# Masks, first products and running sums written into PSUM by ScalarE, products added onto them by TensorE, and a new order of the work

## Chip, cores, metric

One core of one Trainium2 chip. The metric is the device time of one execution in microseconds (us): 423.28 before the change, the median of three runs (422.78 to 424.47).

## What is computed

A layer of an encoder, for 512 tokens of width 1024. Both branches and all gates start from the same normalised input; branch A is latent attention, branch B keeps the best 128 keys of each query by an indexer's scores.

```
h = rmsnorm(x, norm_g)
(q_lat, c_kv, k_rope, z_a, q_b, k_b, v_b, z_b, q_idx, k_idx, w_idx, gate_a, gate_b) = split(h @ w_in)
y_a = mla_attention(q_nope, q_pe, k_nope, k_pe, v_a, pos) * silu(z_a)          # 8 heads, chunk-causal
# branch B: score = sum_h relu(q_idx . k_idx) * w_idx; keys outside the top 128 or the later chunks drop out
logits = q_b . k_sel * scale + rel_bias[t5_bucket(key - query)]                # -inf where not valid
y_b = (softmax(logits) @ v_sel) * silu(z_b)                                    # 8 heads
merged = sigmoid(gate_a) * (y_a @ w_o_a) + sigmoid(gate_b) * (y_b @ w_o_b)
out = rmsnorm(x + merged @ w_out, final_g)
```

## The kernel before, in words

**Arithmetic.** Each fp32 operand is split into a high part, rounded by ScalarE (ACT, line 320 or 329), and a low part, the rest, made by VectorE (DVE, line 346) or GpSimd (POOL, line 348). A product of two operands is three matmuls onto one PSUM bank (`mm3`, line 422; all matmuls at line 418): high by high, low by high, high by low. There are 8 PSUM banks `ps`, each 128x512 fp32. Transposes are at line 435, branch A's logits at lines 1582 to 1584, the indexer's scores at line 883.

**Products in sevens.** Some 2x2 block products are made with seven half-size products in place of eight (`seven`, line 1105): two 512-wide projections as one pair (`proj2`, 84 matmuls of 256 columns in place of 48 of 512), branch B's values (`values2`, the tile `vv`) and the output product (`output`, line 1990, its right operands `s_wo` made by `out_job`). A plain 512-wide projection (`proj`) is 24 matmuls of 512 columns. Before, product 1 goes to SBUF and DVE makes the running sums: u2 is product 6 + product 1, u3 is product 7 added in the bank, then again + product 1; products 5 and 4 go to banks of their own and DVE adds them (`add`).

**Branch B's heads.** `dsa_base` loads a head's bias table and DVE (5 times POOL) adds each tile of `mask` to it, into the tile `s_p`. `mask` holds 0 or -1e30, is made from the top-128 search on DVE (lines 905, 906), and has widths 128 to 512 for the four query tiles. `dsa_head` makes the logits on TensorE into a fresh bank (`qhi` by `s_op`); one DVE instruction at line 1662 adds bank and `s_p` and takes the minimum of the negative; ACT takes the exponent; the rows are normalised, transposed (`s_ph`) and multiplied by `vv`.

**The order.** All engines run lists written at build time. `Flow` (line 140) is a planner: threads ask for steps, banks and slots; at each turn it issues the step that can start first by its own table of costs, with a preference for steps whose operands have been ready for some time (`SETTLE`, line 266), ties broken by a seeded draw (`DRAW`, line 264). `QUEUE` (line 2104) is the list of projection jobs: `ga`, `gb` gates, `za`, `zb`, `ma`, `pe`, `va`, `VB` values of branch B, `sb` its keys and queries, `ou` preparation of output operands; capital letters mean a product in sevens. `fetcher` loads their weights on SP's queue (SyncE) in this order, with four loads held back by `PASSED`; `splitter` splits them; `multiplier` issues the products. Two `lane` threads run the heads of each branch, two at a time. `branch_out` makes the sixteen outer projections (operands `s_ys`), `merged` the left operands `s_mg` of `output`; `finish`, `finish_twice` and `scale_out` do the last norm.

Of the kernel before, what the change touches and what calls it, by code (L numbers as in the profile page):

```python
# [43 lines left out]
class Buf:  # L44


    def __init__(self, tile, name):
        self.tile, self.name, self.w, self.r, self.written = tile, name, 0.0, 0.0, False
        self.by, self.reads = None, {}

    def __getitem__(self, idx):
        return View(self, self.tile[idx])
# [5 lines left out]

class View:
    def __init__(self, buf, ap):  # L60
        self.buf, self.ap = buf, ap

    def __getitem__(self, idx):
        return View(self.buf, self.ap[idx])
# [16 lines left out]
class Step:  # L81
# [4 lines left out]
    moves = 0.0  # L86
    pair = False
# [12 lines left out]
class Get:  # L100
    def __init__(self, pool, cls=None, cap=None):
        self.pool, self.cls, self.cap = pool, cls, cap
# [7 lines left out]
class Pool_:  # L110
# [5 lines left out]
    def give(self, req):  # L116
        if not self.free or (req.cap is not None and self.used.get(req.cls, 0) >= req.cap):
            return None
        self.free.sort(key=lambda b: max(b.w, b.r))
        self.used[req.cls] = self.used.get(req.cls, 0) + 1  # L120
        b = self.free.pop(0)
# [18 lines left out]
class Flow:  # L140
# [40 lines left out]
    def start(self, step, eng):  # L181
        s = self.free[eng]
        for b in step.ins:
            if not b.written and b not in step.outs:
                return math.inf
            s = max(s, b.w + (RAW_LAG.get(eng, 0.0) if b.by == eng else self.lat(b.by, eng)))
        for b in step.outs:
# [10 lines left out]
    def run(self, stop=None):  # L198
        while self.threads:
# [34 lines left out]
            if eng == "SP":  # L234

                self.free["SP"] = s + 0.05
                self.hw = max(self.hw, s) + (0.65 if step.ins and step.outs else 0.475)
                self.dma = max(self.dma, self.hw + 0.65)

                self.dma += dur * (SLOW if self.dma < 7.3 else 1.0)  # L240
                end = self.dma + (2.2 if step.ins and step.outs else 1.0) + step.late
            else:
# [7 lines left out]
                elif step.moves:  # L250
                    self.dma = max(self.dma, end + 1.0) + step.moves
                    end = self.dma + 1.0
            for b in step.ins:
                b.r = b.reads[eng] = max(b.r, end)
            for b in step.outs:
                b.w = max(b.w, end)
                b.written, b.by = True, eng
            self.advance(t, None)
# [5 lines left out]
DRAW = 53  # L264
# [6 lines left out]
def tile_block(ctx: ExitStack, tc: tile.TileContext, a: dict, out: bass.AP, bias_dram: bass.AP):  # L271
# [25 lines left out]
    ps_bufs = set(id(b) for b in PS.free)  # L297

# [6 lines left out]
    def bank(cls):  # L305
        return Get(PS, cls, {"mm": 3, "lg": 2, "pt": 2, "pv": 1, "e": 6}.get(cls))
# [105 lines left out]

    def mm(ps, pairs, start, stop, more=False):
# [6 lines left out]
        t = len(pairs) * (0.0133 + pairs[0][1].n / 2400)  # L420
        return pe(t, [ps], [v for p in pairs for v in p], emit, len(pairs))
# [8 lines left out]
    def turn(parts):  # L430
# [6 lines left out]
        return pe(0.107 * len(parts), [d for d, _ in parts], [s for _, s in parts] + [ident.all], emit, len(parts))  # L437

    held = []

    def hold(n, emit):

        return lambda: held.append([n, emit])

    def passed():
        for x in list(held):
            x[0] -= 1
            if not x[0]:
                held.remove(x)
                x[1]()  # L450

    def dma(dst, src):
# [5 lines left out]
        return Step([("SP", n / 360000.0, lambda: (nc.sync.dma_start(d, s), passed()))], bufs(dst), bufs(src))  # L458

    def pool_dma(dst, src):  # L460
        s = src.ap if isinstance(src, View) else src
        step = Step([("POOL", 1.03, lambda: nc.gpsimd.dma_start(dst.ap, s))], bufs(dst), bufs(src))
# [21 lines left out]
    def pool_dma_out(dst, src):  # L484
        step = Step([("POOL", 1.03, lambda: nc.gpsimd.dma_start(dst, src.ap))], [], bufs(src))
# [50 lines left out]
    def warm_up():  # L536
# [6 lines left out]
        for i in range(NWARM):  # L543
            step = pe(WARM, [ps.all], [zeros.all], fill(256))
            if i == NWARM - 1:
# [331 lines left out]
    def scores(i):  # L877
        n = P * (i + 1)
        work = mask[i]
        for h in range(NH):  # L880
            yield Until(lambda: h in qs and ks)
            ps = yield bank("lg")
            yield pe(0.005 + n / 2400, [ps.all], [qs[h].all, ks[0].all], lambda: nc.tensor.matmul(  # L883
                ps.tile[:, :n], qs[h].tile[:96, TOK[i]], ks[0].tile[:96, :n], start=True, stop=True))
            yield act(ps[:, :n], ps[:, :n], AF.Relu, scale=RD ** -0.5)
# [1308 lines left out]
```

## Time and profile before

| | |
|---|---|
| median of 3 runs | 423.28 us |
| the profiled execution, its time / its span | 422.78 us / 421.0 us |
| granted TensorE clock, mean | 0.996 |
| busy: PE (matmul) / DVE / ACT / POOL | 414.0 / 373.0 / 267.0 / 122.5 us |
| HBM traffic | 130 GB/s over the span |

PE is TensorE's matmuls, PEld its weight loads, SP the engine that issues most DMAs. A busy PE in the profile is a PE with matmuls in flight: their ends are modelled, so the pace of matmuls is better read from starts of long equal rows than from the busy share. In the rows of the timeline stand start, time, engine, line, operation, tiles and how many instructions were merged, and in square brackets the idle time of the engine before the first and who ended it. A tile's first letters name its use: `s_w` weights, `s_h` normalised input, `s_hs` its block sums, `s_pair` outputs of a pair, `s_xr` the residual.

### The profile page before, as it was taken

The numbers are of one execution on the slowest core, as the hardware profiler recorded it, in microseconds if no ns is written. First come the engines' busy times: TensorE is split into PE (matmuls) and PEld (weight loads), VectorE is DVE, ScalarE is ACT, GpSimd is POOL, SyncE is SP. The second block draws the span as 40 slices with busy tenths as digits, with TensorE's granted clock in tenths as the row PEclk, the third lists the DMA queues.
The fourth block names the chain that finished last, engine by engine and source line by source line (L and its number), as shares of the span: only waits on it lengthen the run. The fifth ranks groups of instructions, "written<-read, shape, count | busy, mean of one in ns | idle before, by whom it ended". The sixth has DMA issues, their size and how long they took to land.

```text
span 421.0 us, 7086 instructions
## 1 busy us (share of the span) xinstructions
PE 414.0 (98%) x2314; PEld 364.2 (87%) x2314; DVE 373.0 (89%) x801; ACT 267.0 (63%) x602; POOL 122.5 (29%) x135
## 2 busy tenths in 40 slices
PE   8999999999999999999999999999999999999994
PEld 7999888888888888888999988998998888888883
DVE  4789889569999999999999999979799758999995
ACT  5787778576764748625568677694598434436724
POOL 0037769543464659400013000200100000120650
PEclk9999999999999999999999999999999999999998
DMA  8983135665266341444652347245541888248305
GB/s 247 387 310 110 48 90 190 180 195 135 75 153 186 88 153 51 114 151 149 148 165 77 103 143 172 77 149 146 136 153 56 281 290 272 90 156 287 147 1 199
DMA packets 30790, 65.89 MB, mean 156 GB/s; under 512 B 4793, under 2 KB 6473, under 8 KB 30753
## 3 DMA queue, kind: packets, MB, share of 16 engines
q1 hardware_dynamic: 28400, 61.79, 47.5%
q10 hardware_dynamic: 1584, 2.49, 1.7%
q0 software_dynamic: 768, 1.15, 1.0%
q8 instruction: 18, 0.29, 0.3%
q14 instruction: 20, 0.16, 0.1%
HBM read 50.49 MB, written 4.21 MB: 130 GB/s over the span
## 4 chain that ended last, share of the span: by engine, by line
PE 97%; DMA 1%; DVE 0%; ACT 0%; issue 0%; SPq 0%; DVEq 0%; ACTq 0%
PE ps L418 88%; PE ps L435 5%; PE ps L1583 1%; PE ps L1584 1%; PE ps L1582 1%; PE ps L883 1%; DMA normg<-norm_g 1%; ACT s_xg L329 0%; DVE s_rg L376 0%; ACT junk L329 0%; PE ps L932 0%; DVE s_w L346 0%; DVE s_rg L357 0%; SPq L458 0%; DVEq L2190 0%
## 5 line engine op out<-in xcount | busy, mean ns | idle before, releaser
L418 PE MATMUL ps<-s_h,s_w 128*128 128x512 f32 (+1 forms) x732 | 169.9, 379 | 0.0
L418 PEld LDWEIGHTS ps<-s_h,s_w 128*128 128x128 f32 x732 | 128.3, 189 | 22.0
L320 ACT CAST s_w<-raw 128x512 fp32r<-128x512 f32 (+3 forms) x124 | 71.9, 593 | 20.2 <-DMA raw<-w_o 9.0
L348 POOL TENSOR_TENSOR s_w<-raw,s_w 128x512 fp32r<-128x512 f32 (+2 forms) x39 | 48.7, 1260 | 46.6 <-ACT s_w L320 42.8
L346 DVE TENSOR_TENSOR s_w<-raw,s_w 128x512 fp32r<-128x512 f32 (+2 forms) x85 | 56.0, 672 | 4.5 <-ACT s_w L320 4.0
L418 PE MATMUL ps<-s_ys,s_w 128*128 128x512 f32 x192 | 43.8, 389 | 0.0
L418 PEld LDWEIGHTS ps<-s_ys,s_w 128*128 128x128 f32 x192 | 36.0, 188 | 7.5
L329 ACT ACTIVATE s_p<-s_p,sm 128x128 f32<-128x128 f32 (+3 forms) x62 | 32.7, 552 | 5.2 <-DVE sm L1662 4.4
L418 PE MATMUL ps<-s_wo,s_mg 128*128 128x512 f32 (+1 forms) x156 | 33.2, 373 | 0.0
L418 PE MATMUL ps<-s_w,s_xg 128*128 128x328 f32 (+1 forms) x192 | 32.7, 324 | 0.0
L418 PEld LDWEIGHTS ps<-s_wo,s_mg 128*128 128x128 f32 x156 | 27.6, 188 | 5.2
L418 PEld LDWEIGHTS ps<-s_w,s_xg 128*128 128x128 f32 x192 | 31.4, 188 | 0.2 <-ACT s_rbc L320 0.2
L346 DVE TENSOR_TENSOR s_ph<-ps,s_ph 128x384 fp32r<-128x384 f32 (+1 forms) x48 | 27.5, 591 | 1.0 <-ACT s_ph L320 0.7
L320 ACT CAST s_ph<-ps 128x384 fp32r<-128x384 f32 (+1 forms) x48 | 23.4, 516 | 6.3 <-PE ps L435 4.9
L329 ACT ACTIVATE s_p<-ps,sm 128x128 f32<-128x128 f32 (+3 forms) x32 | 16.8, 528 | 15.9 <-DVE sm L1565 15.7
L348 POOL TENSOR_TENSOR s_p<-s_bias,mask 128x128 f32<-128x128 f32 (+2 forms) x5 | 4.4, 889 | 75.3 <-DMA s_bias<-bias_scratch 39.7
L905 DVE MAX8 sm<-mask 128x8 f32<-128x384 f32 (+2 forms) x48 | 25.7, 548 | 0.2
L906 DVE MATCH_REPLACE8 mask<-sm,mask 128x384 f32<-128x384 f32 (+2 forms) x48 | 25.8, 540 | 0.0
L418 PE MATMUL ps<-s_ph,vv 128*128 128x512 f32 (+3 forms) x128 | 25.1, 318 | 0.0
L435 PE MATMUL ps<-ident,s_p 128*128 128x128 f32 x160 | 23.1, 273 | 0.0
L418 PEld LDWEIGHTS ps<-s_ph,vv 128*128 128x128 f32 x128 | 21.0, 188 | 2.4
L348 POOL TENSOR_TENSOR s_wo<-raw,s_wo 128x512 fp32r<-128x512 f32 x3 | 13.2, 4416 | 28.3 <-ACT s_wo L320 28.3
(200 smaller groups left out, 768.7 us busy)
## 6 DMA issues: line engine op xcount, KB each, us to landing
raw<-w_out SPq DMA_DIRECT2D x18, 512.0 KB, 3.3
s_op<-s_op SPq DMA_DIRECT2D x36, 128.0 KB, 2.8
raw<-w_ga SPq DMA_DIRECT2D x8, 512.0 KB
raw<-w_gb SPq DMA_DIRECT2D x8, 512.0 KB
raw<-w_o SPq DMA_DIRECT2D x16, 256.0 KB, 3.7
s_xn<-x SPq DMA_DIRECT2D x8, 256.0 KB, 5.5
bias_scratch<-s_sig ACTq DMA_DIRECT2D x8, 256.0 KB, 3.1
raw<-w_za SPq DMA_DIRECT2D x4, 512.0 KB, 4.5
```

The costliest lines, as they stand in the source:

```text
L320: nc.scalar.copy(dst.ap, src.ap)
L329: nc.scalar.activation(dst.ap, src.ap, func, **kw)
L346: opts.append(("DVE", 0.07 + 0.00104 * x.n, lambda: nc.vector.tensor_tensor(dst.ap, x.ap, y.ap, op=op)))
L348: opts.append(("POOL", 0.15 + 0.0021 * x.n, lambda: nc.gpsimd.tensor_tensor(dst.ap, x.ap, y.ap, op=op)))
L418: nc.tensor.matmul(ps.ap, l.ap, r.ap, start=start and i == 0, stop=stop and i == len(pairs) - 1, skip_group_check=more)
L435: nc.tensor.transpose(d.ap, s.ap, ident.tile)
L883: yield pe(0.005 + n / 2400, [ps.all], [qs[h].all, ks[0].all], lambda: nc.tensor.matmul(ps.tile[:, :n], qs[h].tile[:96, TOK[i]], ks[0].til ...
L905: yield Step([("DVE", t, lambda: nc.vector.max(m8.tile, work.tile))], [m8], [work])
L906: yield Step([("DVE", t, lambda: nc.vector.match_replace(work.tile, m8.tile, work.tile, MARK))], [work], [m8])
L1582: nc.tensor.matmul(o, q0[0:100], k0[0:100], start=True, stop=False)
L1583: nc.tensor.matmul(o, q0[0:96], k1[0:96], start=False, stop=False)
L1584: nc.tensor.matmul(o, q1[0:96], k0[0:96], start=False, stop=True)
```

## The change

1. `seven`: ACT copies product 1 from bank x into a second bank y, and TensorE adds product 6 (u2), then product 7 (u3), then product 4 onto y. After each of the three ACT copies y to SBUF. Product 5 goes to bank z between products 1 and 6; DVE only adds u3 to it, and u2 to the bank again after product 3. The order of the products is 1, 5, 6, 2, 7, 4, 3 in place of 1, 6, 2, 7, 5, 4, 3, and the right operands are split in the new order.
2. `output`: the same with two banks each of x and y, one tile of 128 rows after the other (`tile`), in the order 1, 2, 6, 7, 5, 4, 3 in place of 1, 7, 2, 6, 5, 4, 3. A tile starts when all four of its operands are there; before, `product` took them one by one.
3. Branch B: `dsa_base` only loads the bias. For each tile of logits ACT copies `mask` into the bank and the two matmuls add onto it; the DVE instruction with the minimum reads bank and bias.
4. The planner: a bank onto which something is to be added must be one in which matmuls have last written the same columns (`adds`, `fills`, `summed`); in a bank every reader on another engine also counts as something to wait for; other costs for matmuls of few columns, DMAs and their issue; `PASSED` and the held steps go; the input's block sums start one head earlier (`SUMS_AT`).
5. `QUEUE` and `DRAW` are new. The six gates `GB0` to `GB5` are no longer pairs, the keys and queries `SB2` and `SB3` are.

```diff
-        yield from times(1, x)
-        spawn(take("1", act(c22, part(x))), 0)
-        y = yield bank("mm")
-        yield from times(6, y)
+        y = yield bank("mm", (0, part(x).n))
+        yield from times(1, x)
+        spawn(take("1", act(part(y), part(x))), 0)
+        z = yield bank("mm")
+        yield from times(5, z)
         yield Until(lambda: "1" in sums)
-        spawn(take("u2", add(c12, y, c22)), 0)
+        yield from times(6, y, True)
+        spawn(take("u2", act(c12, part(y))), 0)
         yield from times(2, x, True)
         spawn(take("c11", act(c11, part(x)), x), 0)
         yield Until(lambda: "u2" in sums)
         yield from times(7, y, True)
-        spawn(take("u3", add(c21, y, c22), y), 0)
-        z = yield bank("mm")
-        yield from times(5, z)
+        spawn(take("u3", act(c22, part(y))), 0)
         yield Until(lambda: "u3" in sums)
-        spawn(take("c22", add(c22, z, c21)), 0)
-        v = yield bank("mm")
-        yield from times(4, v)
+        spawn(take("c22", add(c22, z, c22)), 0)
+        yield from times(4, y, True)
+        spawn(take("c21", act(c21, part(y)), y), 0)
         yield Until(lambda: "c22" in sums)
-        spawn(take("c21", add(c21, v, c21), v), 0)
         yield from times(3, z, True)
...
-            yield tt(probs[i], backward(bias.all.f[:, :n]), mask[i].all, ALU.add, BOTH)
...
-                p.ap, ps.tile[:, :n], p.ap, op0=ALU.add, op1=ALU.min, scale=-1.0, scalar=-FILL,
+                p.ap, ps.tile[:, :n], backward(bias.all.f[:, :n]).ap, op0=ALU.add, op1=ALU.min, scale=-1.0, scalar=-FILL,
...
-            ps = yield bank("lg")
-            yield mm(ps[:, :nn], [(qb[:, TOK[i]], kh[:, :nn]), (qb[:, TOK[i]], kl[:, :nn])], True, True)
+            ps = yield bank("lg", (0, nn))
+            yield act(ps[:, :nn], mask[i].all)
+            yield mm(ps[:, :nn], [(qb[:, TOK[i]], kh[:, :nn]), (qb[:, TOK[i]], kl[:, :nn])], False, True, True)
...
+            yield is_done(("u2", i))
+            yield from tile(7, i, y[i], left1, 256, True)
+            spawn(partial(i, "u3", ((2 + i, 1),)), -1)
...
-QUEUE = 'ga0 ga1 pe ma0 va0 ga2 za0 ma1 va1 ga3 za1 ma2 ga4 za2 ma3 ga5 za3 sb0 zb0 ga6 ga7 sb1 VB GB0 GB1 sb2 zb1 GB2 GB3 sb3 zb2 GB4 GB5 ou zb3 gb6 ou gb7 ou'
+QUEUE = 'ga2 ma2 ga0 za2 ma0 pe ma1 ga5 ma3 ga6 ga7 va0 za3 va1 za1 ga4 za0 zb1 gb0 ga1 zb2 sb1 zb0 sb0 VB gb6 SB2 gb2 SB3 gb5 gb4 gb3 gb7 ga3 ou zb3 gb1 ou ou'
```

Two places show what moved. The first is PE's list in branch B's values, where product 7 ends (its last rows read `s_hs_2372` and `s_hs_2373`, in the new list `s_hs_2364` and `s_hs_2365`). Before:

```order
L418 MATMUL ps_99<-s_w_2593,s_hs_2372 128x256
L418 MATMUL ps_99<-s_w_2594,s_hs_2372 128x256
L418 MATMUL ps_99<-s_w_2593,s_hs_2373 128x256
L418 MATMUL ps_95<-s_w_2610,s_hs_2065 128x256 [waits Activation_49]
L418 MATMUL ps_95<-s_w_2611,s_hs_2065 128x256
L418 MATMUL ps_95<-s_w_2610,s_hs_2066 128x256
```

Now, at the same place, with the logits of heads 0 and 1 (`qhi`) between the products:

```order
L447 MATMUL ps_93<-s_w_2701,s_hs_2364 128x256
L447 MATMUL ps_93<-s_w_2702,s_hs_2364 128x256
L447 MATMUL ps_93<-s_w_2701,s_hs_2365 128x256
L447 MATMUL ps_97<-s_op_2564,qhi_75 128x384 [waits DVE_49,Activation_49]
L447 MATMUL ps_97<-s_op_2593,qhi_75 128x384
L447 MATMUL ps_94<-s_op_2552,qhi_74 128x512 [waits DVE_49,Activation_49]
L447 MATMUL ps_94<-s_op_2553,qhi_74 128x512
L447 MATMUL ps_93<-s_w_2734,s_h_637 128x256 [waits Activation_49]
L447 MATMUL ps_93<-s_w_2735,s_h_637 128x256 [waits DVE_49]
```

Before, product 5 followed product 7 in another bank (95 after 99). Now product 4 follows product 7 in the same bank 93, four matmuls of logits later, and both pairs of logits wait for ACT.

The second place is ACT's list over the same stretch. Before, with the exponents of head 1 (`s_p_2561` to `2563`) and the casts of weights:

```order
L320 COPY s_pair_2520<-ps_98 128x512 [waits PE_49]
L320 CAST s_w_2650<-raw_66 128x512 [waits DVE_49]
L329 ACTIVATE s_p_2562,sm_83<-s_p_2562,sm_78 128x256 [waits DVE_49]
L329 ACTIVATE s_p_2561,sm_83<-s_p_2561,sm_88 128x128 [waits DVE_49]
L320 CAST s_w_2687<-raw_66 128x512 [waits PE_49]
L329 ACTIVATE s_p_2563,sm_83<-s_p_2563,sm_91 128x512 [waits DVE_49]
```

Now:

```order
L345 COPY s_pair_2597<-ps_99 128x512 [waits PE_49]
L345 CAST s_w_2755<-raw_68 128x512
L345 CAST s_w_2781<-raw_66 128x512 [waits DMAHW4_49]
L345 COPY ps_97<-mask_111 128x384
L345 COPY ps_94<-mask_112 128x512
L354 ACTIVATE s_p_2686,sm_83<-s_p_2686,sm_81 128x256 [waits DVE_49]
L354 ACTIVATE s_p_2685,sm_91<-s_p_2685,sm_82 128x384 [waits DVE_49]
L345 COPY s_pair_2601<-ps_93 128x512 [waits PE_49]
```

The copies of `mask` into banks 97 and 94 stand in ACT's list ahead of two exponents, and the copy of u3 (`s_pair_2601` from bank 93) behind them.

More of the change, by code (lines that the diff above doesn't have):

```diff
@@ L234, in run @@
             if eng == "SP":
[L236 to L241, printed above, removed]
+                both = step.ins and step.outs
+                self.free["SP"] = s + (0.55 if both else 0.46)
+                first = s + (1.2 if both else 1.0)
+                self.dma = max(self.dma, first) + dur * (1.8 if both else 0.935) * (SLOW if self.dma < 7.3 else 1.0)
+                end = max(self.dma, first + dur * (1.8 if both else 1.47)) + LANDING + step.late
             else:
@@ L297, in tile_block @@
     ps_bufs = set(id(b) for b in PS.free)
+    for b in PS.free:
+        b.bank = True
     def in_ps(v):
@@ L435, in emit @@
                 nc.tensor.transpose(d.ap, s.ap, ident.tile)
[L437 to L450, printed above, removed]
+        step = pe(0.109 * len(parts), [d for d, _ in parts], [s for _, s in parts] + [ident.all], emit, len(parts))
+        step.fills = [(d, True) for d, _ in parts]
+        return step
     def dma(dst, src):
@@ L1927, in scale_out @@
             spawn(part_out(1, 0, 512, ("ACT", "DVE"), "SP"), 0)
-    def product(n, banks, left, cols, more=False):
-        for k in range(4):
-            yield Until(lambda: k in left and (n, k) in right)
-            for i in range(2):
-                x = cut(left[k], slice(cols + i * P, cols + i * P + P))
-                yield mm3(banks[i].all, x, whole(right[n, k]), k == 0 and not more, k == 3, more)
-            put(*right[n, k])
     def z_parts(z, i):
@@ L1946, in get_banks, with tile @@
                 group.append((yield bank("o")))
-        def keep_half(ps, dst, i, release):
-            s = yield slot("part")
-            yield act(s.all.f, ps.all, AF.Copy, scale=0.5)
-            if release:
-                put(ps)
-            dst[i] = s
-        one, seven = {}, {}
+        def tile(n, i, ps, left, cols, more=False):
+            yield Until(lambda: all(k in left and (n, k) in right for k in range(4)))
+            for k in range(4):
+                c = slice(cols + i * P, cols + i * P + P)
+                yield mm3(ps.all, cut(left[k], c), whole(right[n, k]), k == 0 and not more, k == 3, more)
@@ L1956, in output, with used, copied @@
+        def used(n, left=None):
+            for k in range(4):
+                put(*right[n, k])
+                if left:
+                    put(*left[k])
+        def copied(key, dst, ps, scale=None):
+            yield act(dst, ps.all, AF.Copy, scale=scale)
+            done.add(key)
         yield Until(lambda: 0 in left1)
-        yield from get_banks(x)
-        yield from product(1, x, left1, 0)
         for i in range(2):
-            spawn(keep_half(x[i], one, i, False), 0)
-        yield from get_banks(w)
@@ L1962, in output @@
[L1962 to L1984 removed]
+            x.append((yield bank("o")))
```

178 lines of the change are left out of this document (99 added, 79 removed).

## The prediction

> **What bounds the kernel now.** I read the page's list of engines first, then the chain that ended last, then who PE waited for, then PE's own pace.
>
> ```profile
> PE 414.0 (98%) x2314; PEld 364.2 (87%) x2314; DVE 373.0 (89%) x801; ACT 267.0 (63%) x602; POOL 122.5 (29%) x135
> PE 97%; DMA 1%; DVE 0%; ACT 0%; issue 0%; SPq 0%; DVEq 0%; ACTq 0%
> ```
>
> The chain is 97% PE. A chain that is one engine can still hold hidden waits, so the next rows are all of PE's waits, and two long pieces of the chain.
>
> ```profile
> PE ps L541 <- DVE neghalf L492: 1.1, 1, 1.1
> ...
> 5.34 22.09 PE ps L418 x139
> ...
> 319.61 95.61 PE ps L418 x446
> ```
>
> PE waited once, for 1.1 us, for the zeros of its warm-up. From 5.34 to 319.61 + 95.61 = 415.2 us nothing stopped it. DVE is nearly full too (89%), but nobody on the path waits for it. So the time is: some 5 us ahead of the real matmuls, 410 us of matmuls without a gap, and a tail:
>
> ```profile
> 409.41 5.80 PE L418 MATMUL ps<-s_wo,qhi 128*128 128x512 f32 x36
> ...
> 415.31 0.38 ACT L329 ACTIVATE junk<-ps 128x256 f32<-128x256 f32 x1 [1.00 <-PE ps L418]
> ...
> 415.81 0.42 DVE L357 SCALAR_TENSOR_TENSOR s_rg<-ps,s_fg 128x256 f32<-128x256 f32 x1 [0.18 <-ACT junk L329]
> ...
> 416.88 0.36 ACTq L1917 DMA_DIRECT2D out<-s_rg  x1
> ```
>
> The tail is the last bank's square sum on ACT, weighting on DVE and the store, which ends at 421.0: 5.8 us after the last matmul. A change can win only by fewer or shorter matmuls or at the two ends; it loses by every wait it gives PE.
>
> **The change, part by part.**
>
> *Matmuls.* Three pairs of gates are dissolved: 3 x 84 = 252 matmuls of 256 columns become 6 x 24 = 144 of 512. Two pairs of keys and queries are formed: 96 of 512 become 168 of 256. In all 84 fewer of 256 columns and 48 more of 512; every other product keeps its count. The pace of both, from runs of equal rows:
>
> ```profile
> 204.33 3.04 PE L418 MATMUL ps<-s_w,s_h 128*128 128x256 f32 x24
> 207.20 3.04 PE L418 MATMUL ps<-s_w,s_hs 128*128 128x256 f32 x24
> ...
> 337.80 22.38 PE L418 MATMUL ps<-s_ys,s_w 128*128 128x512 f32 x98
> ```
>
> Starts 2.87 us apart for 24 give 0.1196 us per 256 columns; 22.38 us for 98 give 0.228 us per 512. The sum: 48 x 0.228 - 84 x 0.1196 = 10.94 - 10.05 = **+0.89 us**, all on the path. [...]
>
> *Product 4 behind product 7 in the same bank* (`seven`, three times). Before, products 5 and 4 had banks of their own. Now product 4 may start only when ACT has copied u3 out of the bank, and no product of its own lies between. The price of that turn, with these copies:
>
> ```profile
> L320 ACT COPY s_pair<-ps 128x256 f32<-128x256 f32 x6 | 2.2, 367 | 0.4 <-PE ps L418 0.3
> ...
> L320 ACT COPY s_pair<-ps 128x512 f32<-128x512 f32 x2 | 1.2, 587 | 3.2 <-PE ps L418 3.2
> ```
>
> The tail's 36 matmuls need 12 x 0.228 + 24 x 0.1196 = 5.61 of the row's 5.80 us, so a result leaves PE 0.2 us after its turn; ACT starts 0.1 us later (415.21 to 415.31); for ACT back to PE no row stands, and I take 0.1 too. The turn is 0.4 + 0.59 = 0.99 us for the values, 0.4 + 0.37 = 0.77 for a pair. The cover is what the new list puts between: for the values two matmuls of 384 (0.174 each, midway between the two paces) and two of 512, 0.80 us; for the first pair two of 128 (at half the pace of 256 or, as eight transposes of 128 take 0.87 us below, at 0.11) and two of 384, about 0.5; for the second pair eight of 128 to 384, about 1.0.
>
> ```profile
> 45.17 0.87 PE ps L435 x8
> ```
>
> What shows is 0.2 + 0.25 + 0 = **+0.45 us** if ACT is free at that moment. If it has just begun another instruction, each of the three grows by up to 0.6, so the bounds are 0 and 2.2 us. [...] Behind the waiting matmul PE's whole list waits, since it runs in order. Product 6 onto the copy of product 1 has product 5 as cover (12 matmuls of 256, 1.4 us, in a pair; twice that for the values), product 7 after u2 has product 2, and the additions to bank z have product 4: nothing.
>
> *Masks.* DVE loses 27 sums, POOL 5, and ACT gains 32 copies from SBUF to PSUM.
>
> ```profile
> L346 DVE TENSOR_TENSOR s_p<-s_bias,mask x27: 276/541/1634, 211.1 to 295.3; 128x384 f32<-128x384 f32 x8, 128x256 f32<-128x256 f32 x7, 128x512 f32<-128x512 f32 x7, 128x128 f32<-128x128 f32 x5
> ...
> L329 ACT ACTIVATE ps<-ps 128x512 f32<-128x512 f32 x8 | 4.6, 581 | 1.1 <-PE ps L883 1.1
> ...
> L329 ACT ACTIVATE ps<-ps 128x384 f32<-128x384 f32 x8 | 3.8, 470 | 0.2 <-PE ps L883 0.2
> ...
> L329 ACT ACTIVATE ps<-ps 128x256 f32<-128x256 f32 x8 | 3.0, 378 | 1.4 <-PE ps L883 1.4
> ```
>
> The sums, some 27 x 0.54 = 15 us of DVE, were hidden: worth 0. No row shows a copy into PSUM from SBUF; the nearest are ACT's rewrites in PSUM, and with 0.28 for 128 columns on the same slope the 32 cost 8 x (0.58 + 0.47 + 0.38 + 0.28) = 13.7 us of ACT. ACT has room for them, in the stretch of branch B's heads:
>
> ```profile
> 211.00:265.00 54.00, 54.00 (x370) 50.03 (x369) 52.02 (x118) 39.81 (x94) 5.06 (x6) 1.00 0.45 132
> 265.00:330.00 65.00, 65.00 (x409) 58.77 (x408) 57.35 (x128) 48.39 (x112) 4.54 (x4) 1.00 0.43 129
> ```
>
> The fourth pair of figures is ACT: 88.2 of 119 us, 74%; with the copies 102, or 86%. In the new list PE works on gates and pairs between the logits, and that hides a copy as long as ACT comes in time. Bounds on PE's path: 0, and 13.7 us with no cover at all. I take 0: before, PE waits by semaphore for ACT's casts all over its list, and the trace has not one such wait. A mask must also be there sooner: by the rows below the top-128 search ended at 207 us, and in the new list the first logits come some 10 us of matmuls later than before, so that is covered.
>
> ```profile
> L906 DVE MATCH_REPLACE8 mask<-sm,mask x48: 397/542/678, 100.7 to 206.8; 128x384 f32<-128x384 f32 x16, 128x512 f32<-128x512 f32 x16, 128x256 f32<-128x256 f32 x16
> ```
>
> *The output product.* Product 7 waits for the copy of u2; between lies product 6's other tile, 12 x 0.228 = 2.7 us against a turn of about 1.0 (0.4 + 0.6). Product 4 has product 5 as cover. Product 2 moves from third to second: the last left operand it needs used to have products 1 and 7, 11 us, and now has product 1 alone, 5.5 us. DVE needs for it:
>
> ```profile
> 381.51 0.68 DVE L357 SCALAR_TENSOR_TENSOR s_sig<-s_sig,ps 128x512 f32<-128x512 f32 x1
> ...
> 384.25 0.68 DVE L346 TENSOR_TENSOR s_mg<-s_sig,s_mg 128x512 fp32r<-128x512 f32 x1
> ```
>
> From the first to the end of the second are 3.4 us, so 2 us are left. All this is 0, with a bound of about 2 us if DVE comes late.
>
> *Order.* PE's list is the same, but for names, for the first 45 us, so the head stays; the tail's chain is unchanged. The other queues change: SP's loads of weights go in the new order and four are no longer held; the busy DMA share is under a half and PE never waited for one, so 0, and 1 us if one comes late.
>
> The sum: 0.89 + 0.45 = 1.34 us. For the profiled execution, 421.0 of span and 1.8 around it, 422.78 + 1.34 = 424.1. The median lies 0.5 above it: 423.28 + 1.34 = **424.6 us**.
>
> **The rivals.**
>
> *ACT's list comes late for the masks* (slower). Place: the logits of branch B, from some 213 us on. An ACT list runs in order, and copies now stand among exponents that wait for DVE. For it: ACT at 86%. Against it: gates between. If half of the 32 are late by half an ACT instruction (0.25 us), 16 x 0.25 = 4.0: 423.28 + 1.34 + 4.0 = 428.6. It decides from 0.8 us on, three late copies, where the sum reaches +0.5%. Chance 0.2.
>
> *The ends or the pace get shorter* (faster). DVE has less to do, and PE's paces could rise a little: if all 1118 matmuls of 512 won 2 ns, 2.2 us: 422.4. Even that is no gain beyond 0.5%, for there is nothing else to remove. Chance below 421.2: 0.03.
>
> *The output's turn fails*: product 2 or 7 waits up to 2 us: 426.6. Against it: DVE has less work everywhere. Chance 0.05.
>
> **How the numbers follow.** The forecast's own case, 0.72, runs from 423.3 (paces and turns as good as they can be) to 425.4. A measurement of this kernel tells about 0.5% from no change, 2.1 us: faster is below 421.2, slower above 425.4. Slower takes the two rivals on that side, partly: 0.22; faster 0.03; same 0.75. The range holds 8 in 10 with the lower end 0.7 below the forecast's case (the paces) and the upper end at two thirds of the first rival: 422.6 to 427.4.
>
> **What would show it.** Right: PE's busy time and chain some 1 us longer, no wait of PE but short ones at product 4, ACT up by about 10 us, DVE down by 15 or more, the tail 5.8 us. Wrong: waits of PE for ACT at the logits of branch B (first rival), a gap of PE between the outer projections and product 2 or 7, or a span under 420 us, which would mean that the paces above are not what matmuls cost.

## The result and the profile after

The changed kernel takes 427.82 us (median of 5 runs, 427.60 to 429.56), the kernel before, measured beside it, 424.06 (422.78 to 424.66): slower by 1.0%, ratio 1.010 with a 95% interval of 1.0072 to 1.0128. A later series (run 13) gave 428.58 against 423.76, ratio 1.0101 (1.0082 to 1.0119). The forecast was 424.6, its range 422.6 to 427.4. The profiled execution took 427.66 us, its span is 425.9; before it was 422.78 and 421.0, so 4.9 us are to be found.

First the same two lines of the page: busy time of each engine, and the chain of work that ended last, by engine.

```profile
PE 416.4 (98%) x2278; PEld 363.5 (85%) x2278; DVE 353.9 (83%) x753; ACT 279.4 (66%) x638; POOL 110.0 (26%) x126
PE 38%; DVE 4%; ACT 1%; issue 0%; DVEq 0%; ACTq 0%
```

What the change did to the engines came as forecast: DVE is down by 19 us, ACT up by 12, and PE has 36 matmuls fewer. But the chain is no longer one engine. Its shares add up to 43% only, because it could be followed back from the end no further than 238.66 us, so the 38% is not to be set against the 97% of before. Down to 259.65 us it is PE alone; there it goes over to ACT and DVE:

```profile
238.66 1.13 DVE s_w L371 x2
...
259.65 11.94 PE ps L447 x71
```

PE's waits show this place and two earlier ones.

```profile
PE ps L904 <- DVE s_lat L382: 1.3, 1, 1.3
PE ps L561 <- DVE neghalf L512: 1.1, 1, 1.1
PE ps L447 <- ACT s_pair L345: 0.7, 1, 0.7
PE ps L904 <- DMA s_qs<-s_th: 0.5, 1, 0.5
```

Before there was only the second one, the warm-up. Now there are three more, 2.5 us: the indexer's scores (line 904) wait for DVE and then for a DMA, and a product waits for ACT's copy of a running sum (`s_pair`). The windows say where: PE was not busy for 2.87 us of the first 97 (before 97.00 - 95.82 = 1.18) and for 0.80 of the window from 211 us (before 0). In these rows the first figure behind the window is its length, the next PE's busy time. Before:

```profile
0.00:97.00 97.00, 95.82 (x538) 86.22 (x539) 74.16 (x143) 71.34 (x165) 48.84 (x69) 1.00 0.62 196
```

After:

```profile
0.00:97.00 97.00, 94.13 (x502) 84.20 (x503) 70.73 (x135) 71.07 (x163) 56.54 (x73) 1.00 0.64 201
...
211.00:265.00 54.00, 53.20 (x376) 49.39 (x376) 41.82 (x88) 39.99 (x96) 6.65 (x5) 1.00 0.40 119
```

The tail has not changed: the last 36 matmuls end at 414.27 + 5.80 = 420.07, and the span 5.8 us later, as before.

```profile
414.27 5.80 PE L447 MATMUL ps<-s_wo,qhi 128*128 128x512 f32 x36
```

The largest wait, in order of time on the three engines that make it:

```profile
49.56 2.26 POOL L404 TENSOR_SCALAR s_latraw<-s_latraw,sm 128x384 f32<-128x384 f32 x4
...
51.91 1.59 POOL L373 TENSOR_TENSOR s_tmp<-s_tmp,ropes 32x512 f32<-32x512 f32 x1
...
53.51 0.87 PE L447 MATMUL ps<-s_h,s_w 128*128 128x512 f32 x3
53.54 0.68 DVE L371 TENSOR_TENSOR s_tmp<-s_tmp,s_tmp 32x512 f32<-32x512 f32 x1 [1.17 <-POOL s_tmp L373]
54.25 1.41 DVE L382 SCALAR_TENSOR_TENSOR s_lat<-ps,glat,s_lat 128x512 fp32r<-128x512 f32 x2
55.72 0.39 PE L904 MATMUL ps<-s_qs,s_qs 96*128 96x256 f32 x1 [1.33 <-DVE s_lat L382]
```

POOL scales the raw latents and then takes 1.59 us for a rope product; DVE waits 1.17 us for that; behind it in DVE's list stand the low parts of two latents; they free the bank that the next scores matmul is written into; and PE's list stops at that matmul. By the starts, three matmuls of 0.228 from 53.51 would let the next one start at 54.19, and it starts at 55.72: 1.53 us lost, 0.2 more than the idle that the view gives.

The second place is in the first pair of keys and queries (`SB2`). ACT's list while PE waits for the copy of u3 (the third row):

```profile
258.21 0.51 ACT L354 ACTIVATE s_p<-s_p,sm 128x256 f32<-128x256 f32 x1
...
258.72 0.61 ACT L345 CAST s_w<-raw 128x512 fp32r<-128x512 f32 x1
259.23 0.37 ACT L345 COPY s_pair<-ps 128x256 f32<-128x256 f32 x1
...
259.65 1.69 PE L447 MATMUL ps<-s_h,s_w 128*128 128x256 f32 x12 [0.68 <-ACT s_pair L345]
```

Product 7 was over by about 258.3. The copy began at 259.23, because an exponent and a cast of weights stood ahead of it in the list.

### The profile page after: what moved, and what is told of

It is laid out like the page before. It is cut to its first block, busy times and chain, and to the rows that moved or that the text cites. A ratio compares the mean times of both kernels' runs of the same rounds, so it can differ in the third digit from the quotient of the medians.

```text
span 425.9 us, 6974 instructions
## 1 busy us (share of the span) xinstructions
PE 416.4 (98%) x2278; PEld 363.5 (85%) x2278; DVE 353.9 (83%) x753; ACT 279.4 (66%) x638; POOL 110.0 (26%) x126
## 5 line engine op out<-in xcount | busy, mean ns | idle before, releaser
L447 PE MATMUL ps<-s_h,s_w 128*128 128x512 f32 (+1 forms) x744 | 177.5, 384 | 0.7 <-ACT s_pair L345 0.7
L447 PEld LDWEIGHTS ps<-s_h,s_w 128*128 128x128 f32 x744 | 132.5, 188 | 24.7 <-ACT s_pair L345 1.0
L345 ACT CAST s_w<-raw 128x512 fp32r<-128x512 f32 (+2 forms) x122 | 70.5, 593 | 17.7 <-DVE raw L371 6.1
L373 POOL TENSOR_TENSOR s_w<-raw,s_w 128x512 fp32r<-128x512 f32 (+2 forms) x42 | 51.5, 1233 | 109.8 <-ACT s_w L345 68.4
L371 DVE TENSOR_TENSOR s_w<-raw,s_w 128x512 fp32r<-128x512 f32 (+2 forms) x80 | 51.8, 658 | 9.0 <-ACT s_w L345 8.3
L354 ACT ACTIVATE s_p<-s_p,sm 128x512 f32<-128x512 f32 (+3 forms) x54 | 29.5, 558 | 4.6 <-DVE sm L1676 2.7
L447 PE MATMUL ps<-s_ph,vv 128*128 128x512 f32 (+3 forms) x128 | 27.2, 324 | 0.0
L466 PEld LDWEIGHTS ps<-ident,s_p 128*128 128x128 f32 x160 | 19.4, 140 | 3.6
L345 ACT CAST s_wo<-s_wsum 128x512 fp32r<-128x512 f32 x16 | 9.8, 622 | 15.9 <-DVE s_wsum L371 15.9
```

Source lines behind the costliest of these rows:

```text
L345: nc.scalar.copy(dst.ap, src.ap)
L354: nc.scalar.activation(dst.ap, src.ap, func, **kw)
L371: opts.append(("DVE", 0.07 + 0.00104 * x.n, lambda: nc.vector.tensor_tensor(dst.ap, x.ap, y.ap, op=op)))
L373: opts.append(("POOL", 0.15 + 0.0021 * x.n, lambda: nc.gpsimd.tensor_tensor(dst.ap, x.ap, y.ap, op=op)))
L447: nc.tensor.matmul(ps.ap, l.ap, r.ap, start=start and i == 0, stop=stop and i == len(pairs) - 1, skip_group_check=more)
L466: nc.tensor.transpose(d.ap, s.ap, ident.tile)
```

## The experiments

Sixteen kernels in four series, five rounds each; before took 423.6 to 423.8 in all of them. Where an edit only holds back the issue of some instructions (the number of a step of the plan, and the step behind which it goes), all other rows of all lists are word for word those of the changed kernel.

**1. Some instructions let past others.**

```diff
-            emit()
+            n, self.count = self.count, self.count + 1
+            if n in HOLD:
+                self.held.setdefault(HOLD[n], []).append(emit)
+            else:
+                emit()
+            for late in self.held.pop(n, ()):
+                late()
...
+HOLD = {346: 360, 358: 363, 381: 382, 467: 469}
```

> The changed kernel with five instructions let past others in the lists of VectorE, ScalarE, TensorE and SyncE, all else word for word the same: the low parts of two latents go ahead of the rope's sum on VectorE, one scores matmul goes behind three matmuls of a latent product, one load of gate weights goes behind two DMAs of indexer queries. Theory 'the new order': the two waits of the indexer's scores (excess 1.51 us at 53.7 and 0.65 at 75.3, by starts of matmuls) go, and nothing is late behind them: 427.8 - 2.2 = 425.6 us, 424.9 to 426.3. Rival 'the next thing is late anyway': the waits move to the products of the latents or to later scores, and the time stays within 0.5 of 427.8.

Measured: 429.61 us (428.49 to 432.84). PE's waits:

```profile
PE ps L455 <- POOL s_w L381: 1.5, 1, 1.5
...
PE ps L1606 <- issue: 0.8, 1, 0.8
```

The rival was right: the bank came free sooner (DVE's two low parts began at 53.58 us, in the first profile at 54.25), and now the latent's product waits as long at the same place (1.5 us, there 1.3) for POOL's low part of its weights. The wait is not one instruction in a bad place; nothing is ready there. Two waits that the first profile did not have came as well, one at branch A's first logits (near 93 us) and one of 0.5 us in the output product (near 401 us). For the first the profile names no releaser (`issue`); the logits' operands are put together by DMAs just before, so I take it for a wait for these. The scores' wait at 75 us, which the edit aims at too, did not show; but it did not show in run 2 either, which leaves those rows alone, so that this tells nothing.

**2. Copies of u2 and u3 from a constant table.**

```diff
-        spawn(take("u2", act(c12, part(y))), 0)
+        spawn(take("u2", other(act(c12, part(y)), c12)), 0)
...
-        spawn(take("u3", act(c22, part(y))), 0)
+        spawn(take("u3", other(act(c22, part(y)), c22)), 0)
```

`other` leaves the copy in its place in ACT's list and lets it read a table in SBUF (`ropec`).

> The changed kernel in which ScalarE's copies of u2 and u3 in the three products in sevens read a constant table in SBUF in place of the bank, so that products 7 and 4 wait for no copy; the order of every list is the same. It leaves out the running sums of these three products (their outputs are wrong). Theory 'turns in one bank': the gaps ahead of products 7 and 4 go, 0.94 + 0.38 + 0.21 us by starts of matmuls, some 1.4 us in all: 426.4 us. Rival 'my estimate of the turns': 0.45 us, 427.4. Rival 'something else is late at the same places': within 0.3 of 427.8.

Measured: 426.99 us (426.82 to 428.58). The waits of products 7 and 4 are gone, and right behind them, where there was none, logits wait for a copy of the mask:

```profile
260.01 0.37 ACT L345 COPY ps<-mask 128x256 f32<-128x256 f32 x1
260.44 0.50 PE L447 MATMUL ps<-s_op,qhi 128*128 128x256 f32 x2 [0.76 <-ACT ps L345]
```

So ACT is late by nearly as much for whatever PE wants from it next: the mechanism of the third theory. By its time the run does not tell the three apart; 426.99 lies between the first (426.4) and the second (427.4).

**3. No masks.**

```diff
-            yield act(ps[:, :nn], mask[i].all)
-            yield mm(ps[:, :nn], [(qb[:, TOK[i]], kh[:, :nn]), (qb[:, TOK[i]], kl[:, :nn])], False, True, True)
+            step = act(ps[:, :nn], mask[i].all)
+            step.options = [(*step.options[0][:2], lambda: None)]
+            yield step
+            step = mm(ps[:, :nn], [(qb[:, TOK[i]], kh[:, :nn]), (qb[:, TOK[i]], kl[:, :nn])], True, True, True)
...
```

The copy keeps its step in the plan, so the order stays, but nothing is issued for it.

> The changed kernel without the 32 copies of the mask into PSUM; the logits' first matmul starts the bank, and the order of every list is otherwise the same. It leaves out branch B's mask. Theory 'the copies are hidden': ScalarE's busy time falls by some 13.7 us and the time stays at 427.8, give or take 0.5. Rival 'ScalarE's list comes late for the masks' (the first rival of the prediction): 4 us less, 423.8. A small side effect is possible: with ScalarE freer the copies of u3 come sooner, which would take up to 1.0 us from the turns.

Measured: 428.37 us (427.10 to 429.18): no gain, as the theory had it. But the side effect was real. Without the copies ACT comes to the copy of u3 in time, and product 4 starts without a wait:

```profile
259.63 0.37 ACT L345 COPY s_pair<-ps 128x256 f32<-128x256 f32 x1
...
260.05 1.21 PE L447 MATMUL ps<-s_h,s_w 128*128 128x256 f32 x8
```

The gain was lost elsewhere in this execution, the slowest of the five: 0.9 us at branch A's first logits, and 0.9 for `s_part` near 400 us. Those places the edit does not touch.

**4. All three edits.** The edits of 1 to 3 in one kernel.

> The three edits together: the five instructions let past others, the copies of u2 and u3 from a constant table, no copies of the mask. It leaves out branch B's mask and the running sums of the products in sevens. Theory 'two waits of the scores, the turns, and matmuls': the gains add up, 427.8 - 2.2 - 1.4 = 424.2 us, and what is left over the kernel before (424.1) is no more than the matmuls' 0.8 us with 0.7 of other small things. Rival 'a common cause, such as a slower pace of all matmuls': at least 1.5 us more than that, 425.7 or above.

Measured: 428.61 us (427.44 to 431.17). The gains did not add up, and there was no slower pace either (by starts, all that lies outside of gaps over 0.15 us grew by 0.3 us over the whole list, beside the matmuls' own change): 1.5 us of waiting for POOL at 54 us, 1.4 us at branch A's logits, 1.0 for `s_part`. Removing a wait at one place in this list let the next late thing show.

**5 and 6. The old sums put back**, in the sevens and the output product (5), in the sevens alone (6).

```diff
-        yield from times(6, y, True)
-        spawn(take("u2", act(c12, part(y))), 0)
+        yield from times(6, y)
...
+        spawn(take("u2", add(c12, y, c22)), 0)
```

> The changed kernel with the sevens and the output product of the kernel before put back (products 5 and 4 in banks of their own, running sums on VectorE); the masks by ScalarE, the new QUEUE, the new draw and the planner stay. The lists are the same as the changed kernel's up to 210 us. Theory 'two causes': the waits behind copies of u2 and u3 go (1.4 us in the sevens, and 0 to 1.2 in the output product, which differs by execution), the waits of TensorE before 100 us stay (2.2 us and more): 427.8 - 1.4 - 0.5 = 425.9, 425.2 to 426.6. Rival 'the new sums hold it all': 423.6 + 0.8 of matmuls = 424.4. Rival 'the masks hold it, late copies only show up elsewhere': 427 or above, with waits for ScalarE at branch B's logits.

> The changed kernel with only the sevens of the kernel before put back; the output product keeps its turns in one bank, all else is as changed, and the lists are the same up to 210 us. Theory 'the output's turn is late in some executions, because its copy of u3 stands in ScalarE's list behind casts that wait for VectorE and a load': TensorE waits 0 to 1.2 us for s_part near 400 us, and the time is 0.3 to 1 us above that of the kernel with the old output product too: 426.6. Rival 'the output product costs nothing': the two are equal within 0.2.

Measured: 429.16 us (428.05 to 430.07) and 428.12 (427.67 to 428.17). PE's wait in the output product of kernel 6:

```profile
PE ps L447 <- ACT s_part L354: 1.4, 1, 1.4
```

None of the three held for 5: the time is over the first two, and the third's waits at branch B's logits did not come. The early wait stayed (1.4 us in both), as the first theory says, and kernel 5 has no `s_part` wait; but what 5 won there it lost in the tail: its last matmul ends at 418.65 (412.85 + 5.80), 7.6 us before the end, where the output product of the change leaves 5.8. One ACT wait in the pairs stayed in both, 0.5 us for another copy (`s_pair`, at 272 us). Kernel 6 shows the output product's wait at its largest, 1.4 us; it took less time than 5, not more, so its theory had the place and not the time.

**7. The kernel before with the new QUEUE and draw.**

```diff
-DRAW = 53
+DRAW = 867
-QUEUE = 'ga0 ga1 pe ma0 va0 ga2 za0 ma1 va1 ...
+QUEUE = 'ga2 ma2 ga0 za2 ma0 pe ma1 ga5 ma3 ...
...
-PASSED = {7: 2, 8: 2, 9: 2, 10: 6}
+PASSED = {}
```

> The kernel before, its code and its planner's costs, with only the QUEUE, the draw and the start of the block sums of the changed kernel (and without the four held loads and the held low part, which are tied to the old QUEUE). Theory 'the order of the jobs': TensorE waits again for scores, latents or DMAs between 45 and 100 us, 1 to 3 us in all: 423.6 + 0.8 + 2.0 = 426.4, 425.4 to 428. Rival 'the forms or the planner's new costs': no such waits, 424.4, 423.9 to 425.

Measured: 435.19 us (433.62 to 435.77). The order, with none of the new forms, brings the early waits (2.0 us at 54, 0.3 behind it), and others later for DVE and ACT, 5.3 us in all; the theory had the place right and the size too small. The draw was made for other code, and the four held loads are gone, so that the sum says little about this change.

**8. More pairs**, on kernel 5 with a QUEUE near the old one (`SB2` and `SB3` beside three pairs of gates).

> A version meant to be faster than both: masks by ScalarE, sevens and output product as before the change, the planner as changed, and a QUEUE near the old one in which SB2 and SB3 are pairs as well as three pairs of gates: against the kernel before, 168 matmuls of 256 columns in place of 96 of 512, 20.1 - 21.9 = -1.8 us. The plan holds one wait of TensorE of 1.7 us near 47 us. Theory 'pairs pay, an order without waits would show it': 423.6 - 1.8 + 1.7 = 423.5 with that wait, 421.8 where it turns out hidden. Rival 'what VectorE and ScalarE do for the pairs is late': 425 or above, with waits between 210 and 330 us.

Measured: 427.75 us (425.79 to 430.49): the rival's time, but not its place. The longest waits are near 48 us (1.3, a gate's product for the low part of its own weights, made by POOL) and at branch A's logits near 124 us (0.6 with no releaser named, 1.3 for a DMA), with none between 210 and 330 us, where the rival has them.

**9 and 10. The forms under the old order.** QUEUE, the planner's costs and the held loads are those of before; in 9 only the masks are new, in 10 masks, sevens and output product.

```diff
-QUEUE = 'ga2 ma2 ga0 za2 ma0 pe ma1 ga5 ma3 ...
+QUEUE = 'ga0 ga1 pe ma0 va0 ga2 za0 ma1 va1 ...
+PASSED = {7: 2, 8: 2, 9: 2, 10: 6}
```

> The kernel before with one form of the change: ScalarE writes the masks into PSUM. QUEUE, the planner's costs, the held loads, the sevens and the output product are those of before; the draw is 229, the one of 240 whose plan leaves TensorE the least idle. Theory 'the masks are hidden': 423.7, the time of before, give or take 0.7, and no wait of TensorE between 45 and 100 us. Rival 'copies late for the logits': 425.5 or above, with waits for ScalarE from 210 us on.

> The kernel before with all three forms of the change (masks, sevens with turns in one bank, output product with turns) and nothing else of it: QUEUE, the planner's costs and the held loads are those of before; the draw is 45, the one of 240 whose plan leaves TensorE the least idle, 1.7 us more than with the masks alone. Theory 'two causes': the waits before 100 us are gone, the turns stay: 423.7 + 1.0 to 2.0 = 425.2. Rival 'the order is all of it': 423.7 to 424.2. Rival 'the forms are all of it': 427 or above.

Measured: 428.20 us (427.16 to 428.46) and 425.84 (425.26 to 426.27), ratio 1.0048 (1.0033 to 1.0063). PE's waits in 10:

```profile
PE ps L448 <- ACT s_pair L346: 0.6, 1, 0.6
PE ps L918 <- DMA s_qs<-s_th: 0.5, 1, 0.5
```

The theory for 10 was right: with the forms, a draw of their own and no new order the kernel takes 2.1 us more, and the wait at 54 us is gone. Not all of the 2.1 are the forms': the DMA wait is the scores', at 67 us. Its ACT wait is branch B's values, with the same picture as above:

```profile
219.66 0.51 ACT L355 ACTIVATE s_p<-s_p,sm 128x256 f32<-128x256 f32 x1
...
220.17 0.61 ACT L346 CAST s_w<-raw 128x512 fp32r<-128x512 f32 x1
220.68 0.58 ACT L346 COPY s_pair<-ps 128x512 f32<-128x512 f32 x1
...
221.31 0.86 PE L448 MATMUL ps<-s_w,s_h 128*128 128x256 f32 x5 [0.62 <-ACT s_pair L346]
```

Kernel 9 has no wait for a copy of a mask and none before 100 us worth speaking of, but it is slower: the rival's time, not its place. It lost at the end: 0.9 us at 411 us for DVE, and a tail of 426.4 - 417.9 = 8.5 us.

```profile
412.00 5.90 PE L448 MATMUL ps<-s_wo,qhi 128*128 128x512 f32 x36 [0.92 <-DVE ps L383]
```

DVE's last weightings come late there. In four of the five kernels with the old output product and a new draw (5, 7, 9, 12) the tail was 7.5 to 8.7 us, in one (8) 5.6, and 5.8 in the kernel before; with the new one it was 5.6 to 5.9 in all twelve, under five draws. No run changes the draw and nothing else, so how much of the time of 9, or of any list with a draw of its own, comes from the draw stays open.

**11. Two weightings held back on DVE.**

```diff
+HOLD = {2280: 2301, 2282: 2303}
```

> The changed kernel with two instructions moved in VectorE's list alone: the weightings of the first two output tiles, which wait for the load of the final norm's weights, go behind the three sums of weights, the low part and the addition that stood behind them. Theory 'the output's turn hangs on that load': no wait of TensorE for s_part near 400 us in any profile, and the time is 427.8 less 0 to 1 us: 427.3; the executions near 429 get fewer. Rival 'it hangs on casts that wait for other loads': the wait near 400 us stays.

What the edit aims at, in kernel 3, where the wait was 0.88 us:

```profile
397.03 1.29 DVE L382 SCALAR_TENSOR_TENSOR s_rg<-s_xr,s_fg 128x512 f32<-128x512 f32 x2 [2.02 <-DMA s_fg<-final_g]
...
400.16 0.62 ACT L345 CAST s_wo<-s_wsum 128x512 fp32r<-128x512 f32 x1 [4.00 <-DVE s_wsum L371]
...
401.21 0.59 ACT L354 ACTIVATE s_part<-ps 128x512 f32<-128x512 f32 x1
401.85 1.42 PE L447 MATMUL ps<-s_wo,s_mg 128*128 128x512 f32 x5 [0.88 <-ACT s_part L354]
```

A load of the final norm's weights lands late, DVE waits 2.0 us for it, the sums of weights behind it are late for ACT's casts, the copy of u3 stands behind these casts, and product 4 waits for the copy. Measured with the weightings moved: no wait for `s_part`, and a new wait of 0.2 us for a low part near 410 us. By itself that proves little, since the first profile and run 2 have no such wait either. Six profiles with the same rows there prove more: where DVE waited 0.7 or 0.8 us for the load (run 2, the changed kernel), PE did not wait; where it waited 1.0, 1.6, 2.0 and 2.2 (runs 1, 13, 3, 4), PE waited 0.5, 0.4, 0.9 and 1.0. The time, 428.82 us (428.07 to 429.20), is no better: the profiled execution had 0.7 at branch A's first logits.

**12. More pairs under the old costs** and with the old sevens and output product.

> The kernel before with the masks by ScalarE, the planner's costs of before, and a QUEUE near the old one with SB2 and SB3 as pairs besides three pairs of gates; draw 403. Against the kernel before: 168 matmuls of 256 columns in place of 96 of 512, 20.1 - 21.9 = -1.8 us. Its plan holds no wait of TensorE after the head. Theory 'pairs pay where nothing waits': 423.7 - 1.8 = 421.9, 421.2 to 422.8. Rival 'engines beside TensorE come late for the two pairs more': 423.7 or above, with waits between 210 and 330 us.

Measured: 425.37 us (424.90 to 427.36). The rival's time, but not its place: one wait of 1.1 us, for the first copies of masks (near 188 us), and a tail of 7.5 us took more than the pairs gave.

**13. The changed kernel again.**

> The changed kernel as it is, once more, on the chip of the three runs below. Theory 'waits for DMAs differ by execution': the median lies within 1 us of 427.8, single executions up to 2 us above the fastest, and the profile shows the wait of the scores near 54 us again (1.3 us), and other sizes at 75, 92 and 400 us than the first profile, which had 0.65, 0 and 0 by starts of matmuls. Rival 'the lists alone set every wait': the same waits with the same sizes, within 0.1.

Measured: 428.58 us (427.34 to 429.22). The waits of its profile:

```profile
PE ps L904 <- DVE s_lat L382: 1.4, 1, 1.4
...
PE ps L904 <- DMA s_qs<-s_th: 1.0, 1, 1.0
PE ps L447 <- ACT s_pair L345: 0.7, 1, 0.7
PE ps L447 <- ACT s_part L354: 0.4, 1, 0.4
```

The theory holds: the waits for engines come back to within 0.1 us (1.3 and 0.7 in the first profile), those that hang on a DMA differ, 0.5 and 1.0 at 75 us, 0 and 0.4 at 400. That is why a single wait of these lists cannot be read off the medians of the other runs.

**14 and 15. The order in two parts**, both with all three forms: the new QUEUE with the old costs (14), the old QUEUE with the new costs (15).

> The three forms, the planner's costs of before, and the new QUEUE with its start of the block sums (no held loads, which are tied to the old QUEUE); the draw is 16, the one of 200 with the shortest plan under jitter. Theory 'the QUEUE brings the early waits': waits of TensorE between 45 and 100 us of 1 us or more, and 425.8 + 0.8 of matmuls + 1.0 = 427.6, about the changed kernel's time. Rival 'the planner's new costs bring them': no more than 0.7 us of waits there, 426.6 or below.

> The three forms, the new costs of the planner (no held loads), and the old QUEUE with its start of the block sums; the draw is 11, the best of 120 by its plan, which still leaves TensorE 6.4 us idle (2.1 at 48 us, 1.1 at 52 us). Theory 'the new costs bring early waits of their own': waits of 1.5 us or more between 45 and 60 us, 428 or above. Rival 'the QUEUE alone brings them': none there, 426 or below.

Measured: 429.51 us (428.60 to 429.91) and 434.59 (434.31 to 436.14). Each half brings an early wait of its own, of 2.0 us for ACT (14) and 2.6 us for POOL (15):

```profile
55.88 0.93 PE L467 MATMUL ps<-ident,s_latraw 128*128 128x128 f32 x4 [1.97 <-ACT s_sig L355]
```

```profile
50.64 1.88 PE L447 MATMUL ps<-s_h,s_w 128*128 128x512 f32 x5 [2.60 <-POOL s_w L373]
```

Both theories were right on the wait, and both rivals (that one half alone brings it) fall. The two waits are not the same one: in 14 PE waits at the latents, as in the changed kernel; in 15 a product of a gate waits for the low part of its own weights. Both kernels took longer than the changed one, and each has its own draw, so that the two halves cannot be added up; 14's time was 1.9 us over its theory's.

**16. What the runs point to**: masks by ACT, the sevens of before, the output product of the change, the old costs, `SB2` and `SB3` as pairs beside three pairs of gates, a QUEUE near the old one (`ga0 za3 va0 pe ga1 ma0 ...`).

> A version meant to beat both: masks by ScalarE, the sevens of before, the output product of the change, the planner's costs of before, SB2 and SB3 as pairs besides three pairs of gates, a QUEUE near the old one, draw 856. Theory 'forms where they cost nothing, pairs where nothing waits': matmuls 1.8 us less than the kernel before, tail 5.8 us, 423.7 - 1.8 = 421.9, and up to 1.5 us of waits for masks or DMAs on top: 421.5 to 423.5. Rival 'a new list brings 2 us of waits of its own, as each of the lists before did': 424 or above.

Measured: 423.28 us (421.95 to 424.49, 12 runs), ratio to before 0.9987 (0.9974 to 1.000), and 5.3 us less than the changed kernel in the same series. Its profile has two waits of PE beside the warm-up, both for ACT, of 0.2 us each. The time is in the theory's range; it is as fast as the kernel before or a little faster, and more than that the runs do not say.

## Why the prediction was wrong, point by point

**What bounds the kernel** was right: PE, and "it loses by every wait it gives PE". The direction follows from that. Two of the sizes in the sum were wrong.

**Order: this is the step that failed.** It says "PE's list is the same, but for names, for the first 45 us, so the head stays" and "PE never waited for one, so 0, and 1 us if one comes late". The first is true, the second is true of the old list, and I took the absence of waits there for slack in the new one. The stretch right behind the 45 us was not compared. There PE waits out the latents with gate matmuls (`s_h`) as filler. Before:

```profile
45.80 1.63 PE L418 MATMUL ps<-s_h,s_w 128*128 128x512 f32 x6
...
47.62 3.67 PE L418 MATMUL ps<-s_h,s_w 128*128 128x512 f32 x15
...
51.87 0.85 PE L418 MATMUL ps<-s_h,s_w 128*128 128x512 f32 x3
...
53.74 3.00 PE L418 MATMUL ps<-s_h,s_w 128*128 128x512 f32 x12
...
57.46 1.54 PE L418 MATMUL ps<-s_h,s_w 128*128 128x512 f32 x6
...
60.74 0.86 PE L418 MATMUL ps<-s_lat,s_w 128*128 128x512 f32 x3
```

After:

```profile
46.26 5.04 PE L447 MATMUL ps<-s_h,s_w 128*128 128x512 f32 x21
...
53.51 0.87 PE L447 MATMUL ps<-s_h,s_w 128*128 128x512 f32 x3
...
55.94 1.55 PE L447 MATMUL ps<-s_lat,s_w 128*128 128x512 f32 x6
```

Before, the gates `ga0` and `ga1` stand first in QUEUE, and PE has 48 such matmuls ahead of the first product of the latents (`s_lat`), the 42 of these rows and three each at 58.96 and 59.83; the latter half runs while the latents are split. After, `ma2`, which needs the latents, stands second, and there are 24. What is missing, 24 x 0.228 = 5.5 us of filler, is a bound for the wait, and 1.5 to 1.7 us of it showed by starts in every profile with this list. The other kernels bear the count out. Eleven profiles have 24 gate matmuls there (the changed kernel, runs 1 to 7, 11, 13 and 14), and in all of them PE waits 1.3 to 2.0 us at this place. Seven have 48 or 72 (the kernel before, 8, 9, 10, 12, 15 and 16), and none of them waits for a latent longer than 0.2 us there; 8 and 15, with the planner's new costs, wait earlier and for something else, the filler's own weights.

The scores' DMA (0 to 1.0 at 75 us) and branch A's first logits (0 to 1.1 near 93 us) belong to the same step: their transfers stand on SP's queue behind other rows now. That this is why they are late is argued, not shown; no run moves these rows alone. In the profiled execution the step is worth 2.2 us by the starts of matmuls, in others 1.5 to 2.9, and not 0. By the medians, the forms under the old order take 425.84 us (run 10) and under the new one 428.58 (run 13): 2.7 us, of which 0.9 are the matmuls; the two have different draws.

**Product 4 behind product 7: the mechanism was right, the size was not.** I had 0.2 + 0.25 + 0 = 0.45. The values and the second pair came so (by starts 0.2, and no wait). The first pair showed 0.7 of idle (0.9 by starts) for product 4, and 0.3 more for product 7 behind u2, which the sum had put at nothing. The 0.77 of a turn assumed that ACT is free "at that moment". In the changed kernel and in run 10 alike it had one exponent and one cast to do first, 0.5 + 0.6 us. The turn itself is short: in run 10 the copy ended at 220.68 + 0.58 = 221.26, and PE started at 221.31. The upper bound (0.6 more for each) held it: 0.25 + 0.6 is about what the first pair's product 4 showed. The value should have lain nearer to it, since the list orders ACT's rows by the planner's costs and not by who waits for them.

**Masks** were 0 as a wait, and the estimate of ACT's work was good: 32 copies at a median of 0.426 us are 13.6 us, against 13.7. From the view of the tile `mask` (shortest, median and longest in ns, first and last start):

```profile
L345 ACT COPY ps<-mask x32: 262/426/596, 222.9 to 323.8; 128x128 f32<-128x128 f32 x8, 128x256 f32<-128x256 f32 x8, 128x384 f32<-128x384 f32 x8, 128x512 f32<-128x512 f32 x8
```

But they are not free. Run 3 shows that the wait for u3 is theirs as well: without them ACT is on time (0.68 us of wait with them, none without). The rival "ACT's list comes late for the masks" named the right engine; neither profile of the changed kernel shows a wait of the logits for a mask, while runs 2 (0.8) and 12 (1.1) do.

**The output product** was 0 with a bound of 2. It showed 0 in one profile, 0.4 in the next, and 0.5 to 1.4 in runs 1, 3, 4 and 6. The rival "The output's turn fails" had the place and the price, but another product: product 4 behind u3, by the chain that run 11 cuts, not 2 or 7. On the other side the new form keeps the tail at 5.8 us under other draws, which the sum had no term for.

**Matmuls** at +0.89: 36 matmuls fewer, as counted, at paces as before (24.48 us for a row of 107 of 512 columns, 0.229 each; starts 2.87 us apart for 24 of 256); the runs do not test this term by itself.

The account of the profiled 4.9 us: 1.7 of idle in the first 97 us, 0.8 from 211 us on, and 2.4 of longer busy time (416.4 against 414.0). By the starts of matmuls, which leave out the modelled ends, it closes better: 0.8 for the matmuls at the paces of before; 3.3 in four gaps, 1.50 at 54 us, 0.65 at 75, 0.28 (product 7) and 0.84 (product 4) at 256 to 259; 0.25 in one gap of the head at 5.3 us; and 0.5 spread over gaps under 0.15 us each. The tail gives nothing, and there is no slower pace among the causes.

## What to carry to other kernels

A bound engine without waits says nothing of how near the others are behind it: when the order changes, look at the new list for the stretches where the bound engine lives on filler, and count the filler there against the old list (here 24 matmuls against 48). A result that passes through another engine in the middle of a sum costs its short copy plus whatever stands ahead of it in that engine's list (here 0.37 us behind 0.51 and 0.61), so price it with one or two instructions ahead and not with an idle engine. And take a wait away only with an idea of what is late next: here runs 1 and 2 only moved the wait, and what worked, in run 16, was a list that had work in hand at every such place (its two waits of PE beside the warm-up are 0.2 us each).

## What I had not expected of the hardware

**A wait of 2 us cost nearly twice.** In run 14 PE idled 1.97 us at 53.9; the granted clock of the stretch fell to 0.76, and six matmuls of 512 columns took 3.18 us. In run 13 it idled 1.40 us at nearly the same place; the clock stayed at 1.00, and six took 1.54. Wait and slower matmuls of run 14 come to 1.97 + 3.18 - 1.54 = 3.6 us. The stretch from 53 to 60 us in run 14, and PE's row of these six:

```profile
53.00:60.00 7.00, 5.03 (x18) 3.43 (x18) 5.54 (x9) 5.36 (x11) 3.25 (x5) 0.76 0.34 111
```

```profile
56.59 3.18 PE L448 MATMUL ps<-s_lat,s_w 128*128 128x512 f32 x6
```

The same two views of run 13:

```profile
53.00:60.00 7.00, 5.60 (x30) 4.42 (x28) 5.58 (x10) 6.44 (x15) 6.78 (x9) 1.00 0.19 63
```

```profile
56.22 1.54 PE L447 MATMUL ps<-s_lat,s_w 128*128 128x512 f32 x6
```

In run 7 a wait of 1.97 us at nearly the same place came with a clock of 0.78 (53.5 to 60.5 us), and in run 8 two waits of 0.55 and 1.25 us within 2.3 us came with 0.81 (122.5 to 129 us). In run 15 the wait of 2.60 us came with 0.94 (40 to 53 us) and 0.87 (53 to 60 us): ten matmuls of 512 columns took 4.01 us right behind it, and ten took 2.57 from 56.53 us on. The wait of the changed kernel, 1.3 us, and those of runs 1 and 4 at this place, 1.5 us, left the clock at 1.00. In run 14 transposes stand right ahead of the wait and behind it, in run 15 plain matmuls, and the clock fell in both. No run changes the length of a wait and nothing else, so what it takes to lower the clock is not shown.

**Waits behind transfers differ between executions.** The profile of the kernel before has no wait of PE behind a DMA, and its times lie within 422.3 to 425.0 in all series. The changed lists have up to three places that, as I read them, hang on one, at 75, 93 and 400 us, and the waits there range from 0 to 1.1 us in profiles of the same rows (0.5 and 1.0 at 75 us in the two of the changed kernel). That they make the times differ is argued, not shown.
